# Both heads' scores in one step, alternating RWKV products, and HGRN2 levels over 128 sources in a two-layer hybrid decoder trunk

## The chip, the cores and the metric

The kernel runs on one core of one Trainium2 chip, as one launch. The metric is the device time of that core in microseconds, the median of several runs. TensorE (PE) multiplies matrices into PSUM, VectorE (DVE) and ScalarE (ACT) work elementwise, GpSimd (POOL) does a few powers and clears, SyncE (SP) issues most of the DMAs.

## The reference

The input is one sequence of 256 tokens by 2048 features in fp32; the trunk has two layers. A layer normalises its input, multiplies it by one combined input projection, runs four groups of 8 heads of 64 features on the result, joins the groups by an output projection, and then runs a SwiGLU feed-forward network (2048 to 5632 and back). Both halves have a norm before and after and a residual. The groups are these:

- **Retention** (RetNet): rotary queries and keys, scores `q k` under a causal decay, scores times values.
- **HGRN2**: a gated linear recurrence. Its scores are

```python
pair = jnp.where(causal, jnp.exp(jnp.minimum(cum[:, :, :, None, :] - cum[:, :, None, :, :], 0.0)), 0.0)
scores = jnp.einsum('bhtd,bhsd,bhtsd->bhts', qc, kc, pair)
```

  so every pair of a target t and a source s has a decay of its own in every feature.
- **mLSTM**: scores `q k` times `exp(logd - m_t)`, with stabilised gates, and a normaliser beside the values.
- **RWKV-7**: a generalised delta rule with one state of 64 by 64 a head:

```python
state = (state * jnp.exp(lwt)[:, :, None, :]
         - jnp.einsum('bhvk,bhk->bhv', state, kkt)[..., None] * (at * kkt)[:, :, None, :]
         + vt[..., None] * kt[:, :, None, :])
return state, jnp.einsum('bhvk,bhk->bhv', state, rt)
```

## The kernel before

**Projections.** All weights are streamed from HBM once, in units of 128 x 1024 elements. `Weights` (line 220 on) loads a unit, ScalarE rounds it to `w_hi` (line 246), and VectorE makes the rest `w_lo` (line 247); splitting runs three units ahead (`NHL`). A product is then made of three TensorE passes in a rounded fp32 format, `w_hi` with `u` and with its low part, `w_lo` with `u`. These are the rows named `acc<-u,w_hi`, `po<-w_lo,m` and so on. All matmuls of the kernel go through the helper `mm`, so they have line 299, and transposes have line 303: rows are told apart by their tiles.

**Mixers.** A pair of heads shares the 128 partitions: head 0 on partitions 0 to 63, head 1 on 64 to 127. There are four such tiles j in each group and layer. The mixers are written as Python generators, `rwkv`, `rw_head`, `rw_tail` for RWKV and `retention`, `hgrn`, `mlstm` for the others (the last three groups run one half group after the other, two tiles at once, in the order of `SEQ`). `interleave` (line 723) is the planner: it walks the projection matmuls in `stream` and, wherever a generator is due, lets it issue its next step. Due times are counted in `self.pe`, the planner's own sum of matmul times, and a generator says by `yield 1.1`, say, how much of it must pass before its next step. Within these steps, the build's scheduler orders each engine's instructions by a simulated timeline, so an instruction that is not ready there lets others pass.

**PSUM.** The eight banks are three for projections (`acc`), two for RWKV (`pr`, handed out in turn by `ret_bank`) and three for the other mixers (`po`, by `oth_bank`). A bank that is handed out again must first have been read out by VectorE or ScalarE.

**The places the change touches.**

- `scores` (line 955) makes one head's 128-source scores: a matmul of 256 target columns for the sources 0 to 127 and one of 128 columns for the rest, with 64 contraction rows. `retention` and `mlstm` call it once a head, with a `yield` between.
- `mlstm` (line 1216) first spreads one row of running maxima over 128 partitions by a matmul of `pick` (64 rows, one column broadcast) with `mrow` (64 x 256): the rows `po<-mlrow,mlpick`. Two operations on VectorE subtract the gate and an exponential on ScalarE gives the decay `Dt`, which is multiplied into the scores.
- `hgrn` (line 1079) builds the scores by levels m = 1, 2, 4 ... 64: a level adds all pairs whose source lies in an even block of m tokens and whose target lies in the odd block behind it, and then folds the decays of its blocks into `q2` and `k`. Up to m = 32 a level has four matmuls, for 64 sources (32 at m = 32) on one half of the output partitions each; VectorE copies what the mask `hm` selects into `P` (line 1118, `copy_predicated`), for m up to 16. At 32 and 64 ScalarE and VectorE copy quarters into place.
- `rwkv` (line 1394) makes the triangular products `BK` with `KVR` head by head into two banks. At its end it makes the outputs `y2` head by head: for each of four chunks n of 64 tokens a product of `G` with `KVT` (128 contraction rows, 64 outputs) and, for n above 0, one of `KVR` with the state `S0` (64 rows, 64 outputs).
- `attend` (line 941) multiplies `P` with the values; `P` has three blocks of 128 targets a head.

Of the kernel before, what the change touches and what calls it, by code (L numbers as in the profile page):

```python
# [18 lines left out]
F32R = mybir.dt.float32r  # L19
# [13 lines left out]
LAT = 1.1  # L33
# [70 lines left out]
HMASK = HLEV[:-2]  # L104


def _constants():
# [31 lines left out]
    tg = lambda m: t64[:, t64[0] // m % 2 == 1]  # L139
    hm = np.stack([np.tile(i // m + 1 == tg(m) // m, 2) for m in HMASK], axis=1)  # L140
# [130 lines left out]
class Trunk:  # L271
# [394 lines left out]
    def mixing(self):  # L666
        tc, nc, A, l = self.tc, self.nc, self.A, self.l
        with ExitStack() as ctx:
# [4 lines left out]
            if l == 0:  # L673
                self.W.advance()
                self.c = self.cp.tile([128, NCST - 128], F32, name="cst")
                nc.sync.dma_start(out=self.c, in_=A["cst"][:, 128:])
                self.hm = self.cp.tile([128, len(HMASK), 64], U32, name="hm")
                nc.sync.dma_start(out=self.hm, in_=A["hmask"])
# [262 lines left out]
    def attend(self, P, v, j, nw=None):  # L941

        pso = self.oth_bank()
        for t in range(2):
            for hh in range(2):
                o, h = slice(64 * hh, 64 * hh + 64), 64 * (2 * (j % 2) + hh)
                if t == 0:
                    self.mm(pso[o, 0:256], v[:, 0, h:h + 64], P[:, hh, 0:256], stop=False)
                else:
                    self.mm(pso[o, 128:256], v[:, 1, h:h + 64], P[:, hh, 256:384], start=False)  # L950
# [4 lines left out]
    def scores(self, q, k, hh):  # L955

        r = slice(64 * hh, 64 * hh + 64)
        ps = self.oth_bank()
        self.mm(ps[:, 0:256], k[r, 0:128], q[r, 0:256])
        self.mm(ps[:, 256:384], k[r, 128:256], q[r, 128:256])  # L960
        return ps

    def oth_tiles(self, t):
# [13 lines left out]
        self.mrow = t([64, 256], "mlrow", F32R)  # L977
        self.act(self.mrow.rearrange("p (a b) -> p a b", b=64), self.zero[0:64].unsqueeze(1).to_broadcast([64, 4, 64]))
        self.pick = t([64, 8], "mlpick", F32R)
        self.tt(self.pick, self.ident[0:64, 0:8], self.ident[0:64, 32:40], ALU.add)  # L980
# [30 lines left out]
    def retention(self, j, qk, v, out):  # L1011
        P, rc = self.P[j % 2], self.rcs[j % 2]
        for hh in range(2):
            ps = self.scores(qk[:, 0, :], qk[:, 1, :], hh)
# [4 lines left out]
            yield LAT if hh else 0.5  # L1019
# [59 lines left out]
    def hgrn(self, j, st, v, out):  # L1079
# [8 lines left out]
        D4 = P[:, :, 128:256].rearrange("p h (t c) -> p h t c", t=2)  # L1088
        side = P.rearrange("p h (b t) -> p h b t", b=3)[:, :, 0:3:2, :]
# [10 lines left out]
        self.mul(D4, self.cst("id64", 64).unsqueeze(1).unsqueeze(1).to_broadcast([128, 2, 2, 64]),  # L1100
                 rc[:, 24:28].rearrange("p (t h) -> p h t", t=2).unsqueeze(3).to_broadcast([128, 2, 2, 64]))
        yield LAT
        E, spare = f, e
        for i, m in enumerate(HLEV):
            nb, w = 128 // m, min(m, 32) if m < 64 else 64
            qv = q2.rearrange("p h (b two m) -> p h b two m", two=2, m=m)
            ps = self.oth_bank()
            if m < 64:
                rows = 64 if m < 32 else 32
                o = ps[:, 0:128].rearrange("p (h t c) -> p h t c", h=2, t=2)  # L1110
# [4 lines left out]
                if m < 32:  # L1115
                    dst = P[:, :, 128:256].rearrange("p h (g two m) -> p h g two m", two=2, m=m)[:, :, :, 1, :]
                    mask = self.hm[:, i, :].rearrange("p (g m) -> p g m", m=m)
                    nc.vector.copy_predicated(dst, mask.unsqueeze(1).to_broadcast([128, 2, 64 // m, m]),
                                              ps[:, 0:128].rearrange("p (h g m) -> p h g m", h=2, m=m))
                else:  # L1120
                    for b in range(2):
                        bs = slice(64 * b, 64 * b + 64)
                        (self.act if b else nc.vector.tensor_copy)(side[bs, :, :, bs], D4[bs])
                        self.act(side[64 * b:64 * b + 32, :, :, 64 * b + 32:64 * b + 64], o[64 * b:64 * b + 32])
            else:
                o = ps[0:64, 0:256].rearrange("p (h t c) -> p h t c", h=2, t=2)
                for t in range(2):
                    self.mm(o[:, :, t, :], k[:, 128 * t:128 * t + 64], q2[:, :, 128 * t + 64:128 * t + 128])
                self.act(side[0:64, :, :, 64:128], o)
# [11 lines left out]
        self.act(P[:, :, 128:256], ps[:, 0:256].rearrange("p (h t) -> p h t", h=2))  # L1141
        yield LAT
        self.attend(P, v, j, self.pcol("hg_nw", j))
# [72 lines left out]
    def mlstm(self, j, qk, v, out):  # L1216
        P, rc = self.P[j % 2], self.rcs[j % 2]
        Dt = self.A2[2 * (j % 2) + 1].rearrange("p a t -> p (a t)")[:, 0:384]
        for hh in range(2):
            h = 2 * j + hh  # L1220
            pm = self.oth_bank()
            self.mm(pm[:, 0:256], self.pick[:, h:h + 1].to_broadcast([64, 128]), self.mrow)
            mp = self.cst("mpos", 384)
# [371 lines left out]
```

## Time and profile before

| | |
|---|---|
| median of 3 runs | 2680.61 us (2678.51 to 2680.84) |
| profiled execution | 2681.49 us, span 2679.7 us |
| TensorE, matmul rows | 2630.9 us, 98%, 17732 rows |
| VectorE | 1698.9 us, 63% |
| ScalarE | 1308.2 us, 49% |
| DMA | 459.04 MB, mean 171 GB/s |
| token mixing with its output projection | about 15 to 591 us and 1346 to 1931 us |
| feed-forward | about 599 to 1340 us and 1938 to 2670 us |

How to read it: a timeline row gives the start in us, the time until the last merged instruction ended, the engine, the line, the operation, `out<-in`, the contraction rows * output columns of the stationary operand, the moving operand's size, and how many instructions are merged. An fp32 matmul has two rows in the trace. Matmul rows overlap, since each lasts from its start until its result is out; what counts for the time is the distance from start to start.

### The profile page before, as it was taken

What the parts mean: (1) busy time and instruction counts of PE and PEld (TensorE: products, weight loads), DVE (VectorE), ACT (ScalarE), POOL (GpSimd) and SP (SyncE); (2) the same over time, 40 slices, a digit from 0 to 9 for tenths busy, and PEclk for the clock granted to TensorE, in tenths of its full rate; (3) what the DMA queues carried; (4) which work ended last, traced back from release to release, by engine and by line L of the source; (5) the groups of instructions that cost most, each with busy time, mean ns of one, the idle gap of its engine ahead of it and who ended that gap; (6) DMA issues with size and microseconds to landing.
All of it is one profiled execution on the core that took longest, in us unless ns stands there. A gap on an engine that the chain in (4) does not pass through costs nothing.

```text
span 2679.7 us, 44884 instructions
## 1 busy us (share of the span) xinstructions
PE 2630.9 (98%) x17732; PEld 2352.7 (88%) x17732; DVE 1698.9 (63%) x3017; ACT 1308.2 (49%) x2169; POOL 67.2 (3%) x129
## 2 busy tenths in 40 slices
PE   7999999999999999999999999999899999999998
PEld 7999999888888888888899999997788888888888
DVE  6877877576555555455578778775765555555444
ACT  5454444466444444444374544544564444444442
POOL 0000000000000000000000000000000000000000
PEclk9999999999999999999999999999899999999999
DMA  6544354556666666666555444545466666666664
GB/s 228 160 136 143 118 154 143 161 167 188 189 188 189 188 188 188 192 199 199 171 164 155 137 135 129 155 141 157 140 187 188 188 188 188 188 189 194 195 203 142
DMA packets 149459, 459.04 MB, mean 171 GB/s; under 512 B 29120, under 2 KB 40064, under 8 KB 149248
## 3 DMA queue, kind: packets, MB, share of 16 engines
q1 hardware_dynamic: 148576, 455.51, 56.5%
q8 instruction: 139, 2.28, 0.3%
q10 hardware_dynamic: 672, 0.66, 0.1%
q14 instruction: 72, 0.59, 0.1%
HBM read 450.61 MB, written 3.41 MB: 169 GB/s over the span
## 4 chain that ended last, share of the span: by engine, by line
PE 98%; DVE 1%; ACT 0%; DMA 0%; issue 0%; POOL 0%; SPq 0%; POOLq 0%; DVEq 0%; ACTq 0%
PE acc L299 56%; PE po L299 28%; PE pr L299 13%; PE pr L303 1%; PE po L303 1%; DVE h L291 0%; DMA h<-in_x 0%; DVE un L287 0%; POOL small L309 0%; SPq L340 0%; ACT junk L294 0%; DVE w_lo L247 0%; DVE u L291 0%; DVE small L291 0%; DVE yw L291 0%
## 5 line engine op out<-in xcount | busy, mean ns | idle before, releaser
L247 DVE TENSOR_TENSOR w_lo<-w_raw,w_hi 128x1024 fp32r<-128x1024 f32 x840 | 1028.2, 1224 | 756.4 <-ACT w_hi L246 745.8
L246 ACT ACTIVATE w_hi<-w_raw 128x1024 fp32r<-128x1024 f32 x840 | 889.0, 1059 | 979.2 <-PE po L299 339.8
L299 PE MATMUL acc<-u,w_hi 128*128 128x256 f32 (+1 forms) x4256 | 999.1, 315 | 0.9 <-DVE u L291 0.9
L299 PE MATMUL acc<-u,w_lo 128*128 128x256 f32 x2656 | 750.0, 284 | 1.1 <-DVE w_lo L247 1.1
L299 PEld LDWEIGHTS acc<-u,w_hi 128*128 128x128 f32 x4256 | 701.5, 191 | 55.9 <-issue 3.3
L299 PEld LDWEIGHTS acc<-u,w_lo 128*128 128x128 f32 x2656 | 505.9, 191 | 7.8 <-DVE w_lo L247 1.3
L299 PE MATMUL po<-u,w_hi 128*128 128x512 f32 x1056 | 384.2, 396 | 0.0
L299 PE MATMUL po<-u,w_lo 128*128 128x256 f32 x1056 | 289.8, 279 | 0.0
L299 PE MATMUL pr<-u,w_hi 128*128 128x512 f32 x704 | 245.6, 396 | 0.0
L299 PEld LDWEIGHTS po<-u,w_hi 128*128 128x128 f32 x1056 | 196.6, 188 | 44.5
L299 PEld LDWEIGHTS po<-u,w_lo 128*128 128x128 f32 x1056 | 199.2, 189 | 3.7
L299 PE MATMUL pr<-u,w_lo 128*128 128x256 f32 x704 | 192.5, 279 | 0.0
L299 PE MATMUL acc<-w_hi,ah 128*128 128x256 f32 (+1 forms) x528 | 177.4, 336 | 0.0
L299 PE MATMUL acc<-w_lo,ah 128*128 128x256 f32 (+1 forms) x528 | 177.4, 336 | 0.0
L299 PE MATMUL acc<-w_hi,al 128*128 128x256 f32 (+1 forms) x528 | 177.4, 336 | 0.0
L299 PEld LDWEIGHTS pr<-u,w_hi 128*128 128x128 f32 x704 | 130.3, 188 | 29.4
L299 PE MATMUL acc<-w_hi,u 128*128 128x256 f32 (+1 forms) x768 | 150.3, 290 | 0.0
L299 PEld LDWEIGHTS pr<-u,w_lo 128*128 128x128 f32 x704 | 132.6, 188 | 2.1
L299 PE MATMUL po<-w_hi,ah 128*128 128x512 f32 (+1 forms) x352 | 127.6, 362 | 0.0
L299 PE MATMUL po<-w_hi,al 128*128 128x512 f32 (+1 forms) x352 | 127.6, 362 | 0.0
L299 PE MATMUL po<-w_lo,ah 128*128 128x512 f32 (+1 forms) x352 | 127.6, 362 | 0.0
L299 PEld LDWEIGHTS acc<-w_hi,u 128*128 128x128 f32 x768 | 120.8, 190 | 4.4 <-issue 2.7
(293 smaller groups left out, 2978.1 us busy)
## 6 DMA issues: line engine op xcount, KB each, us to landing
w_raw<-in_wgu SPq DMA_DIRECT2D x352, 512.0 KB, 4.6
w_raw<-in_win SPq DMA_DIRECT2D x240, 512.0 KB, 4.1
w_raw<-in_wdn SPq DMA_DIRECT2D x132, 512.0 KB, 3.8
w_raw<-in_wout SPq DMA_DIRECT2D x48, 512.0 KB, 3.7
w_raw<-in_wdnn SPq DMA_DIRECT2D x44, 512.0 KB, 3.5
w_raw<-in_woutn SPq DMA_DIRECT2D x16, 512.0 KB
w_raw<-in_wmv SPq DMA_DIRECT2D x8, 544.0 KB, 4.2
bp<-in_bpost SPq DMA_DIRECT2D x32, 128.0 KB, 3.2
```

The source lines that it names most:

```text
L246: self.nc.scalar.activation(hi, t, AF.Copy)
L247: self.nc.vector.tensor_tensor(out=lo, in0=t, in1=hi.bitcast(F32), op=ALU.subtract)
L299: self.nc.tensor.matmul(out, lhsT=lhsT, rhs=rhs, start=start, stop=stop, skip_group_check=True)
L303: self.nc.tensor.transpose(out, a, self.ident[0:n, 0:n])
```

## The change

- `scores` makes both heads at once, into two banks, with the matmuls of head 0 and head 1 alternating. `retention` and `mlstm` call it once a tile, and their waits are joined.
- `mlstm` spreads both heads' rows into one bank first, from `mrow` and `pick` of 128 rows (the rows from 64 on are zero), keeps the decay in `P` itself and makes one exponential of both heads.
- `hgrn` makes every level with two matmuls for all 128 sources, and copies all seven levels by the mask, which now has 128 columns. The copies at 32 and 64 and the clear of a quarter of `P` are gone; the diagonal is written for 256 columns a head. The blocks of `P` are in another order, which `attend` takes into account by `last`.
- `rwkv` alternates the heads in the triangular products, into two banks. It makes the outputs of both heads together: first all eight products with `G`, then all six with `S0`, in an order in which neighbours lie on different halves.

```diff
-HMASK = HLEV[:-2]
+HMASK = HLEV
...
-    tg = lambda m: t64[:, t64[0] // m % 2 == 1]
-    hm = np.stack([np.tile(i // m + 1 == tg(m) // m, 2) for m in HMASK], axis=1)
+    t128 = np.arange(128)[None, :]
+    tg = lambda m: t128[:, t128[0] // m % 2 == 1]
+    hm = np.stack([np.tile(p[:, None] // m + 1 == tg(m) // m, 2) for m in HMASK], axis=1)
...
-    def scores(self, q, k, hh):
-        r = slice(64 * hh, 64 * hh + 64)
-        ps = self.oth_bank()
-        self.mm(ps[:, 0:256], k[r, 0:128], q[r, 0:256])
-        self.mm(ps[:, 256:384], k[r, 128:256], q[r, 128:256])
+    def scores(self, qk):
+        ps = [self.oth_bank() for _ in range(2)]
+        for o, s, t in ((slice(0, 256), slice(0, 128), slice(0, 256)), (slice(256, 384), slice(128, 256), slice(128, 256))):
+            for hh in range(2):
+                r = slice(64 * hh, 64 * hh + 64)
+                self.mm(ps[hh][:, o], qk[r, 1, s], qk[r, 0, t])
         return ps
...
-        self.mrow = t([64, 256], "mlrow", F32R)
+        self.mrow = t([128, 256], "mlrow", F32R)
...
-        self.pick = t([64, 8], "mlpick", F32R)
+        self.pick = t([128, 8], "mlpick", F32R)
...
     def retention(self, j, qk, v, out):
-        for hh in range(2):
-            ps = self.scores(qk[:, 0, :], qk[:, 1, :], hh)
+        for hh, ps in enumerate(self.scores(qk)):
...
-            yield LAT if hh else 0.5
+        yield LAT + 0.5
...
     def hgrn(self, j, st, v, out):
-        with self.behind_norm():
-            nc.gpsimd.memset(side[64:128, :, :, 0:64], 0.0)
...
-                for t in range(2):
-                    for b in range(2):
-                        c, g0 = 128 * t + 64 * b, (128 * t + 64 * b) // (2 * m)
-                        self.mm(o[64 * b:64 * b + rows, :, t, :], k[:, c:c + rows], qv[:, :, g0:g0 + 32 // m, 1, :])
...
+            o = ps[:, 0:256].rearrange("p (h t c) -> p h t c", h=2, t=2)
+            for t in range(2):
+                self.mm(o[:, :, t, :], k[:, 128 * t:128 * t + 128], qv[:, :, 64 // m * t:64 // m * (t + 1), 1, :])
+            dst = P[:, :, 0:256].rearrange("p h (g two m) -> p h g two m", two=2, m=m)[:, :, :, 1, :]
+            mask = self.hm[:, i, :].rearrange("p (g m) -> p g m", m=m)
+            nc.vector.copy_predicated(dst, mask.unsqueeze(1).to_broadcast([128, 2, 128 // m, m]),
+                                      ps[:, 0:256].rearrange("p (h g m) -> p h g m", h=2, m=m))
...
     def mlstm(self, j, qk, v, out):
-        for hh in range(2):
-            h = 2 * j + hh
-            pm = self.oth_bank()
-            self.mm(pm[:, 0:256], self.pick[:, h:h + 1].to_broadcast([64, 128]), self.mrow)
...
-            self.act(Dt, Dt, AF.Exp, scale=-1.0)
-            yield 0.8
-            ps = self.scores(qk[:, 0, :], qk[:, 1, :], hh)
-            self.stt(P[:, hh, :], ps[:, 0:384], HD ** -0.5, Dt, ALU.mult, ALU.mult)
-            yield LAT + 0.5 if hh else 1.0
+        pm = self.oth_bank()
+        for hh in range(2):
+            self.mm(pm[:, 256 * hh:256 * hh + 256], self.pick[:, 2 * j + hh:2 * j + hh + 1].to_broadcast([128, 128]), self.mrow)
...
+        self.act(P, P, AF.Exp, scale=-1.0)
+        yield 1.6
+        for hh, ps in enumerate(self.scores(qk)):
+            self.stt(P[:, hh, :], ps[:, 0:384], HD ** -0.5, P[:, hh, :], ALU.mult, ALU.mult)
+        yield LAT + 1.0
...
     def rwkv(self, j, out):
+        pg = [self.ret_bank() for _ in range(2)]
+        for n in range(4):
+            for hh in range(2):
+                rhs = KVR[half[hh], n, 0:3:2, :] if hh == 0 else KVR[half[hh], n, 1:3, :]
+                self.mm(pg[hh][:, 128 * n:128 * n + 128], BK[half[hh], n].rearrange("p s t -> p (s t)"), rhs)
         for hh in range(2):
-            ps = self.ret_bank()
-            for n in range(4):
-                rhs = KVR[half[hh], n, 0:3:2, :] if hh == 0 else KVR[half[hh], n, 1:3, :]
-                self.mm(ps[:, 128 * n:128 * n + 128], BK[half[hh], n].rearrange("p s t -> p (s t)"), rhs)
...
-        for hh in range(2):
-            y2 = self.ret_bank()[:, 0:128].rearrange("p (t e) -> p t e", t=2)
-            for n in (2, 3, 0, 1):
-                o = y2[half[n % 2], n // 2, :]
-                self.mm(o, G[:, hh, n, 64:128], KVT[:, n, hh, :], stop=n == 0)
-                if n > 0:
-                    self.mm(o, KVR[half[hh], n, 2, :], S0[half[hh], n, :], start=False)
+        y2 = [self.ret_bank()[:, 0:128].rearrange("p (t e) -> p t e", t=2) for _ in range(2)]
+        place = lambda n, hh: y2[hh][half[n % 2], n // 2, :]
+        for n, hh in ((0, 0), (1, 0), (0, 1), (1, 1), (2, 0), (3, 0), (2, 1), (3, 1)):
+            self.mm(place(n, hh), G[:, hh, n, 64:128], KVT[:, n, hh, :], start=n < 2, stop=n == 0)
+        for n, hh in ((2, 0), (3, 1), (2, 1), (3, 0), (1, 1), (1, 0)):
+            self.mm(place(n, hh), KVR[half[hh], n, 2, :], S0[half[hh], n, :], start=False)
```

More of the change, by code (lines that the diff above doesn't have):

```diff
@@ L676, in mixing @@
                 nc.sync.dma_start(out=self.c, in_=A["cst"][:, 128:])
-                self.hm = self.cp.tile([128, len(HMASK), 64], U32, name="hm")
+                self.hm = self.cp.tile([128, len(HMASK), 128], U32, name="hm")
                 nc.sync.dma_start(out=self.hm, in_=A["hmask"])
@@ L939, in finish, with attend @@
         self.mul(out, t1, psb[:, 0:256])
-    def attend(self, P, v, j, nw=None):
+    def attend(self, P, v, j, nw=None, last=2):
         pso = self.oth_bank()
+        P3 = P.rearrange("p h (b t) -> p h b t", b=3)
         for t in range(2):
@@ L947, in attend @@
                 if t == 0:
-                    self.mm(pso[o, 0:256], v[:, 0, h:h + 64], P[:, hh, 0:256], stop=False)
+                    self.mm(pso[o, 0:256], v[:, 0, h:h + 64], P3[:, hh, 0:2] if last == 2 else P3[:, hh, 0:3:2], stop=False)
                 else:
-                    self.mm(pso[o, 128:256], v[:, 1, h:h + 64], P[:, hh, 256:384], start=False)
+                    self.mm(pso[o, 128:256], v[:, 1, h:h + 64], P3[:, hh, last], start=False)
         sq, t1, _ = self.scr[j % 2]
@@ L975, in oth_tiles @@
         self.ms = t([128, 6, 16], "mlstats")
[L977 to L980 removed]
+        self.mrow = t([128, 256], "mlrow", F32R)
+        self.act(self.mrow.rearrange("p (a b) -> p a b", b=64), self.zero.unsqueeze(1).to_broadcast([128, 4, 64]))
+        self.pick = t([128, 8], "mlpick", F32R)
+        self.tt(self.pick, self.ident[:, 0:8], self.ident[:, 32:40], ALU.add)
         self.mlv = t([128, 2, 4, 65], "mlv")
@@ L1085, in hgrn @@
         P, rc = self.P[j % 2], self.rcs[j % 2]
-        D4 = P[:, :, 128:256].rearrange("p h (t c) -> p h t c", t=2)
-        side = P.rearrange("p h (b t) -> p h b t", b=3)[:, :, 0:3:2, :]
-        with self.behind_norm():
-            nc.gpsimd.memset(side[64:128, :, :, 0:64], 0.0)
+        near = P[:, :, 0:256].rearrange("p h (t c) -> p h t c", t=2)
         for hh in range(2):
@@ L1099, in hgrn @@
         nc.vector.tensor_copy(rc[:, 24:28], ps[:, 0:4])
-        self.mul(D4, self.cst("id64", 64).unsqueeze(1).unsqueeze(1).to_broadcast([128, 2, 2, 64]),
-                 rc[:, 24:28].rearrange("p (t h) -> p h t", t=2).unsqueeze(3).to_broadcast([128, 2, 2, 64]))
+        self.mul(near, self.ident.unsqueeze(1).unsqueeze(1).to_broadcast([128, 2, 2, 128]),
+                 rc[:, 24:28].rearrange("p (t h) -> p h t", t=2).unsqueeze(3).to_broadcast([128, 2, 2, 128]))
         yield LAT
@@ L1104, in hgrn @@
         for i, m in enumerate(HLEV):
-            nb, w = 128 // m, min(m, 32) if m < 64 else 64
+            nb = 128 // m
             qv = q2.rearrange("p h (b two m) -> p h b two m", two=2, m=m)
             ps = self.oth_bank()
-            if m < 64:
-                rows = 64 if m < 32 else 32
-                o = ps[:, 0:128].rearrange("p (h t c) -> p h t c", h=2, t=2)
-                for t in range(2):
-                    for b in range(2):
-                        c, g0 = 128 * t + 64 * b, (128 * t + 64 * b) // (2 * m)
-                        self.mm(o[64 * b:64 * b + rows, :, t, :], k[:, c:c + rows], qv[:, :, g0:g0 + 32 // m, 1, :])
[L1115 to L1129, printed above, removed]
+            o = ps[:, 0:256].rearrange("p (h t c) -> p h t c", h=2, t=2)
[5 more added lines that the diff above has]
+                                      ps[:, 0:256].rearrange("p (h g m) -> p h g m", h=2, m=m))
             Ev = E[:, 0:2 * nb].rearrange("p (b two) -> p b two", two=2)
@@ L1140, in hgrn @@
         self.mm(ps[:, 0:256], k[:, 0:128], q2[:, :, 128:256])
-        self.act(P[:, :, 128:256], ps[:, 0:256].rearrange("p (h t) -> p h t", h=2))
+        self.act(P[:, :, 256:384], ps[:, 0:256].rearrange("p (h t) -> p h t", h=2))
         yield LAT
-        self.attend(P, v, j, self.pcol("hg_nw", j))
+        self.attend(P, v, j, self.pcol("hg_nw", j), last=1)
         yield LAT
```

12 lines of the change are left out of this document (6 added, 6 removed).

## Prediction, made before the result was known

> **What bounds the kernel now.** I read the page first, then the waits of TensorE, then the busy times of the two token-mixing stretches.
>
> ```profile
> span 2679.7 us, 44884 instructions
> PE 98%; DVE 1%; ACT 0%; DMA 0%; issue 0%; POOL 0%; SPq 0%; POOLq 0%; DVEq 0%; ACTq 0%
> PE po L303 <- DVE un L287: 27.9, 5, 13.0
> PE pr L303 <- DVE kap L287: 3.2, 1, 3.2
> PE acc L299 <- DVE w_lo L247: 1.1, 1, 1.1
> sum 840.00, PE 840.00 PEld 787.93 DVE 653.99 ACT 414.43 POOL 45.74; mean PE 420.00 PEld 393.96 DVE 326.99 ACT 207.21 POOL 22.87
> HBM read 450.61 MB, written 3.41 MB: 169 GB/s over the span
> ```
>
> The chain that ended last is TensorE for 98% of the span. Its largest wait, 27.9 us for `un`, lies at the norms, which the change does not touch. For split weights (`w_lo`) it waited 1.1 us in all. The sum row is over both token-mixing stretches (60 to 480 and 1400 to 1820): TensorE is busy without a gap, VectorE 654 of 840 us, ScalarE half. So the projection matmuls always have their operands, and every mixer block between them pushes them back by its own length. A TensorE microsecond saved in a block is a microsecond of span, as long as VectorE keeps up.
>
> **How a block is priced.** A block is a run of mixer matmuls between two projection matmuls. Each fp32 matmul leaves two records. The timeline of TensorE around one head's RWKV output products:
>
> ```profile
> 190.61 0.28 PE L299 MATMUL acc<-u,w_hi 128*128 128x256 f32 x1
> 190.82 0.33 PE L299 MATMUL pr<-KVT,G 128*64 128x64 f32 x2
> 191.08 0.33 PE L299 MATMUL pr<-S,KVR 64*64 64x64 f32 x2
> ...
> 191.85 0.34 PE L299 MATMUL pr<-KVT,G 128*64 128x64 f32 x4
> 192.37 0.39 PE L299 MATMUL acc<-u,w_hi 128*128 128x256 f32 x1
> 192.59 0.28 PE L299 MATMUL acc<-u,w_lo 128*128 128x256 f32 x1
> 243.44 0.68 PE L299 MATMUL pr<-TDD,LoT 64*64 64x64 f32 x16
> 244.05 0.44 PE L303 MATMUL po<-ident,A 128*128 128x128 f32 x2
> ```
>
> Projection matmuls of 256 columns start 0.12 us apart. Here the block starts 0.21 after the last one (0.09 too late), and the first one after it takes 0.22 (0.10 too much): a block of another tile shape costs 0.19 besides its own length. This head: 192.37 − 190.82 + 0.19 = 1.74 us. It has 14 records, but 0.26 passes from group to group, with two records or four: it pays for its five changes of shape, not for work. The last two rows are the opposite: 16 records of one shape, heads alternating, take 0.61, so a step of two records costs about 0.06.
>
> **RWKV output products** (end of `rwkv`). Two heads, four tiles, two layers: 16 blocks of 1.74 now, 3.48 a tile. The change issues 8 products with `G` (16 records, neighbours in different column halves), then 6 with `S0` (12 records, different row halves), into two banks. By the 16-record row: 0.61 + (0.61 − 2 × 0.06) + 0.19 = 1.29, so 2.19 saved a tile, 17.5 us over eight. Where the last chunk's values come late the block will break in two and pay entry, exit and a shape change again; I take half the tiles broken at about 0.25 each: **−16.5**. Lower bound: if the second bank is not free, each head goes alone with its own products grouped, two runs near 0.39 (the 8-record row below) + 0.19 = 0.97, 1.94 a tile: −12.3. The last tile of layer 1 also stands on the chain ahead of the 3.2 us wait for `kap`; it gains the same there.
>
> **RWKV's triangular products** (`BK` with `KVR`), heads alternating instead of one after the other:
>
> ```profile
> 93.64 1.71 PE L299 MATMUL pr<-KVR,BK 64*128 64x128 f32 x16
> 95.28 0.39 PE L299 MATMUL acc<-u,w_lo 128*128 128x256 f32 x1
> 54.68 0.70 PE L299 MATMUL pr<-X,wa 64*128 64x256 f32 x4
> 55.31 0.51 PE L299 MATMUL acc<-u,w_hi 128*128 128x256 f32 x2
> 169.04 0.70 PE L299 MATMUL pr<-X,wa 64*128 64x256 f32 x2
> 169.66 0.39 PE L299 MATMUL acc<-u,w_lo 128*128 128x256 f32 x1
> ```
>
> `X,wa` is the test that the kernel already contains: two matmuls on different row halves into two banks. Together, four records take 0.63; one alone takes 0.62. The second head is free when it stands beside the first. In the triangular block 16 records take 1.64. At 0.11 a record (full-shape rows below) plus 0.2 of filling and draining they would need 1.96 in a row, so about three of eight steps overlap already; alternating needs 8 × 0.11 + 0.2 = 1.08. Saved 0.56 × 8 = 4.5 at most, nothing if the second bank comes late; both heads stand in one block now, so I take **−4.0**.
>
> The Trainium skill, TensorE: Matmul & The Clock Gate, Part 3, says that matmuls keep program order in start and end. By that rule two heads issued one after the other would share nothing, and alternating would save 8 × 0.11 = 0.88 a tile, 7.0 us. The 1.64 here is too short for it, so the row decides.
>
> **Scores and decay rows.**
>
> ```profile
> 224.47 0.92 PE L299 MATMUL po<-A 64*128 64x256 f32 x4
> 225.32 0.39 PE L299 MATMUL acc<-w_lo,u 128*128 128x256 f32 x1
> 225.75 0.38 PE L299 MATMUL po<-mlrow,mlpick 64*128 64x256 f32 x1
> 226.06 0.39 PE L299 MATMUL acc<-w_hi,u 128*128 128x256 f32 x1
> 480.39 0.93 PE L299 MATMUL po<-A 64*128 64x256 f32 x8
> 481.25 0.39 PE L299 MATMUL acc<-u,w_lo 128*128 128x256 f32 x1
> ```
>
> The first is one mLSTM head, 0.85 + 0.19 = 1.04. The x8 row is a retention pair whose two heads already run side by side in 0.86 + 0.19 = 1.05. So retention has most of this gain: **−0.8**, between 0 and −1.6. For mLSTM's eight pairs, 2 × 1.04 becomes 1.05 where both banks are free: 8.2 us at most. But the ring has three banks, the decay rows of both running pairs take two of them, and each head's bank must first be read out by VectorE (four operations a pair). Where one head comes first, the schedule sends it alone, as in the `X,wa` row at 169.04. I take a third: **−2.5**, between 0 and −8.2.
>
> The decay rows (`mlpick`) go from 64 to 128 rows, the shape of the projections: 0.31 + 0.19 = 0.50 alone now, afterwards 0.12 like a projection matmul. Some stand beside scores and cost less, so I put the sixteen at 0.38: **−4.2**, between −3 and −6.1. In exchange the exponential now waits for both heads' four operations on VectorE; behind it on ScalarE stand the `w_hi` of later units, and ScalarE has half its time free.
>
> **HGRN2's levels.** Now four matmuls a level on 64 column halves, 8 records; afterwards two on the full shape, 4 records.
>
> ```profile
> 109.92 0.46 PE L299 MATMUL po<-A,A 128*64 128x64 f32 x8
> 110.31 0.50 PE L299 MATMUL acc<-u,w_hi 128*128 128x256 f32 x2
> 139.42 0.65 PE L299 MATMUL po<-A,A 128*64 128x128 f32 x4
> 140.00 0.39 PE L299 MATMUL acc<-w_hi,u 128*128 128x272 f32 x1
> 155.68 0.38 PE L299 MATMUL pr<-KVT,KBT 128*128 128x128 f32 x2
> 155.90 0.38 PE L303 MATMUL po<-ident,A 128*128 128x128 f32 x2
> 156.04 0.38 PE L299 MATMUL acc<-w_lo,u 128*128 128x272 f32 x1
> 156.26 0.41 PE L299 MATMUL acc<-w_hi,u 128*128 128x272 f32 x2
> ```
>
> A small level costs 0.39 + 0.19 = 0.58 alone; the level of 64 costs 0.58 + 0.19 = 0.77. Four full-shape fp32 records cost 0.36 and, with no late entry, 0.09 after them (0.22 in place of 0.13, these projections having 272 columns): 0.45, 0.11 each in the array. With 0.55 for six levels (two pairs' levels sometimes share a block) a pair now pays 4.07 and will pay 7 × 0.45 = 3.15: **−7.4** over eight pairs; between 0 (levels always shared) and −8.8.
>
> What VectorE gets in exchange:
>
> ```profile
> L1118 DVE COPY_PREDICATED P<-hm,po x40: 278/301/496, 113.0 to 1618.1; 128x128 f32<-128x128 uint32 x40
> L278 DVE TENSOR_TENSOR P<-cst,rc x8: 404/412/420, 112.0 to 1600.0; 128x256 f32<-128x256 f32 x8
> L1123 DVE COPY P<-P x8: 276/278/281, 132.1 to 1619.4; 64x256 f32<-64x256 f32 x8
> sum 158.00, PE 158.00 PEld 142.40 DVE 136.95 ACT 65.63 POOL 2.27; mean PE 39.50 PEld 35.60 DVE 34.24 ACT 16.41 POOL 0.57
> ```
>
> The last row sums the four stretches in which the small levels run (109 to 145, 266 to 312, 1437 to 1473, 1593 to 1633): VectorE is busy 137 of 158 us. The masked copies go from 5 of 128 columns a pair, about 0.35 each, to 7 of 256. Their price is bounded by 0.35 + 0.14 = 0.49 (an estimate: the tensor operations' slope per 128 columns) and by twice, 0.70. With the copy of 0.28 gone and the diagonal doubled (0.41 to about 0.68) that adds 8 × 1.7 = 13 to 8 × 3.1 = 25 us, while TensorE leaves 7.4 less: 150 to 162 us of work in 150.6. At the lower price it just fits; at the upper 11.5 us are missing. What is late next is `w_lo`, three units ahead. I take **+3**, between 0 and +11.5.
>
> Costed at nothing: the fewer ScalarE copies and the dropped clear on GpSimd, which are off the chain, and the zero rows of `mlrow`, written before the first projection ends. The mask grows from 160 to 448 KB on SP's queue; behind it stand `wa`, `gup`, `gb` and the later weight units. The units requested ahead of it cover it; at the mean rate of 169 GB/s it would cost 1.7 us once without them. The planner charges an fp32 matmul by 4 × max(rows out, columns), which comes to the same per level, per score and per product before and after, so the projections keep their places beside the mixers.
>
> **The sum.** −16.5 − 4.0 − 0.8 − 2.5 − 4.2 − 7.4 + 3 = −32.4 us. The profiled execution took 2681.5 (span 2679.7): 2649.1. It stands 0.9 above the median of 2680.6, so the forecast is **2648**. All upper bounds without the VectorE loss give −46.7, 2634.
>
> **Rivals.**
> 1. *The second bank is late everywhere*: alternation exists only in the program's text. Rows at 169.04 speak for it, the x8 and x4 rows against. Scores and triangular products gain nothing, the output products only their grouping: −12.3 − 4.2 − 7.4 + 3 = −20.9, 2660.
> 2. *VectorE becomes the bound in the HGRN2 stretches* at 0.70 a copy: −35.4 + 11.5 = −23.9, 2657. For it: 137 of 158; against it: `w_lo` waits of 1.1.
> 3. *The late entry and exit belong to fp32, not to the shape*; then full-shape levels pay 0.19 too and give up the column halves. The array's own time doubles from 4 steps of 0.06 to 4 of 0.11 on 48 levels, +0.2 × 48 = 9.6 in place of −7.4: −15.4, 2665. The row at 155.90 speaks against it. The Trainium skill, TensorEngine Tiling (Array Packing), Performance Considerations, points this way: with a stationary free size up to 64 it wants column tiling.
> 4. *Slower*: the masked copy of 256 columns from PSUM costs far more than twice. The 56 copies are in VectorE's order ahead of `w_lo`. The need is 137 + 56c − 14 (what is dropped of today's copies, net of the diagonal) against 150.6; it eats the whole 35.4 from c = 1.13 us; at 1.25 the shortage is 42, +7, 2688. Nothing in the copies' 0.28 to 0.50 suggests it.
>
> **How the numbers follow.** Forecast 0.63, rivals 0.17, 0.11, 0.06 and 0.03. The range 2632 to 2664 reaches from the upper bounds past rivals 1 and 2. Faster by over 0.2%, about what a measurement of this kernel tells from no change: 0.96; within: 0.01, between rivals 3 and 4; slower: 0.03, rival 4.
>
> **What would show it.** Output products in blocks of some 28 records near 1.1 us, not two of 1.55; `mlpick` rows of 128*128 without a late entry; level rows of 128*128 x4; `KVR,BK` near 1.1. If mLSTM's `po<-A` rows stay x4, the banks were late. If TensorE waits for `w_lo` appear in the four stretches, rival 2 or 4 holds. A copy above 0.7, or new waits over 10 us elsewhere, would make the prediction wrong.

## The result and the profile after

| | before | after |
|---|---|---|
| median | 2680.32 us (2678.51 to 2680.84) | 2666.59 us (2664.78 to 2668.22) |
| span of the profiled execution | 2679.7 us | 2664.2 us |
| TensorE, matmul rows | 2630.9 us, 17732 | 2608.6 us, 17540 |
| VectorE | 1698.9 us | 1705.3 us |
| ScalarE | 1308.2 us | 1297.5 us |

The change makes the kernel faster: the ratio is 0.995, with an interval of 0.9933 to 0.9967, or 13.7 us. The forecast was 32.4 us, and the time lies 2.6 us above the end of the range. A layer's token mixing, with its output projection, can be counted from the wait for `un` that opens the layer to the wait for `un` behind its output projection (12.95 to 585.81 and 1334.62 to 1924.80 us in before, 12.42 to 584.89 and 1333.13 to 1909.54 in after). So counted, layer 1 became 13.8 us shorter and layer 0 only 0.4, although both run the same code. Something in layer 0 eats most of what the parts gain there.

The chain of waits in after, by engine:

```profile
PE 96%; DVE 2%; DMA 1%; issue 0%; ACT 0%; POOL 0%; SPq 0%; POOLq 0%; DVEq 0%; ACTq 0%
```

TensorE's share of the chain falls from 98 to 96%; VectorE's rises from 1 to 2 and that of DMA from 0 to 1%. The waits of TensorE in after (line, tile, what it waited for, us in total, how often, the longest):

```profile
PE po L304 <- DVE un L288: 27.8, 7, 12.4
PE pr L304 <- DVE kap L288: 7.0, 2, 3.8
PE acc L300 <- ACT m L295: 4.4, 2, 2.2
PE acc L300 <- DVE w_lo L248: 1.0, 2, 0.8
PE pr L300 <- DVE KVT L287: 0.9, 2, 0.5
```

and the row of the same view of before that the prediction doesn't show:

```profile
PE acc L299 <- ACT m L294: 2.2, 1, 2.2
```

The norms' wait for `un` is what it was, and `w_lo` is in time. But `kap` and `m` were waited for once and are now waited for twice: before, this pair of waits stood in layer 1 alone. The windows around the end of the mixers show the same (us, busy time of TensorE, weight loads, VectorE, ScalarE, GpSimd, granted TensorE clock, DMA share, GB/s), first before, in layer 0 and in layer 1:

```profile
480.00:560.00 80.00, 80.00 (x405) 65.56 (x405) 46.99 (x85) 38.15 (x70) 5.64 (x5) 1.00 0.58 169
1840.00:1880.00 40.00, 33.84 (x159) 26.77 (x158) 18.53 (x30) 13.90 (x23) 1.48 (x2) 0.87 0.50 145
```

then after, in layer 0 and in layer 1:

```profile
480.00:560.00 80.00, 72.82 (x356) 60.15 (x355) 40.46 (x75) 33.89 (x65) 3.95 (x5) 0.94 0.51 149
1780.00:1870.00 90.00, 83.42 (x512) 67.85 (x511) 49.63 (x89) 38.02 (x60) 3.94 (x5) 0.94 0.50 145
```

In layer 0, TensorE worked through the 80 us before; now it is idle for 7.2 of them, at a mean clock of 0.94. The timeline of TensorE in after at that place (start, length, the wait and its releaser in brackets; a few rows are enough):

```profile
526.26 0.39 PE L300 MATMUL po<-w_lo,m 128*128 128x512 f32 x1
526.49 0.62 PE L300 MATMUL po<-w_hi,m 128*128 128x512 f32 x2
526.94 0.40 PE L300 MATMUL po<-w_lo,m 128*128 128x512 f32 x1
...
527.82 0.43 PE L300 MATMUL pr<-F,TT 128*128 128x64 f32 x2 [0.31 <-DVE F L279]
...
529.77 0.45 PE L300 MATMUL pr<-KVT,G 128*64 128x64 f32 x8 [0.50 <-DVE KVT L287]
...
535.44 0.66 PE L304 MATMUL pr<-ident,kap 128*128 128x128 f32 x2 [3.77 <-DVE kap L288]
538.32 1.65 PE L300 MATMUL acc<-w_hi,m 128*128 128x512 f32 x3 [2.21 <-ACT m L295]
...
541.47 0.63 PE L300 MATMUL acc<-w_lo,m 128*128 128x512 f32 x1
541.90 0.63 PE L300 MATMUL acc<-w_hi,m 128*128 128x512 f32 x1
...
542.70 0.63 PE L300 MATMUL acc<-w_hi,m 128*128 128x512 f32 x2
```

From 526.94 to 538.32 no projection matmul starts; this is the dry stretch, as it is called from here on. TensorE does the last steps of the last RWKV tile one after the other, each of which waits for an elementwise operation on its result. The output projection needs that tile in its last units and has nothing else to do. The chain of work through the same place, in order of time:

```profile
528.23 1.23 DVE w_lo L248
529.49 0.24 DVE KVT L287
529.77 0.84 PE pr L300 x14
...
533.46 1.05 POOL rwc L310
534.53 0.77 DVE kap L288 x3
```

The last two rows belong to `rw_tail`: mean and variance, a power on GpSimd, the scalings of `kap`, then the transposes. A weight split of 1.23 us even stands in VectorE's order ahead of the last `KVT`. The wait isn't all of the price. The windows give the granted clock (the figure after GpSimd's):

```profile
529.00:532.00 3.00, 1.79 (x22) 1.05 (x20) 1.56 (x5) 0.53 (x3) 0.00 (x0) 1.00 0.59 198
532.00:533.00 1.00, 0.00 (x0) 0.00 (x0) 0.00 (x0) 1.00 (x8) 0.00 (x0) 0.69 0.49 197
535.00:542.00 7.00, 4.34 (x11) 3.28 (x12) 2.71 (x7) 1.15 (x2) 0.00 (x0) 0.50 0.00 0
```

The clock falls from 1.00 to 0.50 between 532 and 533 us, early in the wait of 3.77 us: TensorE's last row ended at 531.68 (530.98 + 0.70), and in the 3 us before 532 it was busy for 1.79. It is still 0.50 when the work comes back, and projection matmuls that started 0.23 us apart (526.26, 526.49) start 0.43 apart (541.47, 541.90) until 542.70. The Trainium skill, TensorE: Matmul & The Clock Gate, Part 1, says that the clock is halved after an idle window of about 3.4 us and comes back after about as long a time of sustained work. The trace agrees on the way back, with 4.4 us of matmuls at half clock after 538.32; on the way down it does not, for no idle stretch of 3.4 us stood ahead of the fall. By an estimate from these rows the dry stretch costs about 10 us: 11.4 us without a projection matmul, less some 3 of mixer work that had to be done anyway, plus about 2 for ten matmuls at half clock.

Why it is late is seen in the order. The build fixes TensorE's order, and the trace repeats it. Projection and feed-forward matmuls that stand ahead of the first transposes of the tail of the last RWKV tile:

| | layer 0 | layer 1 |
|---|---|---|
| the place where the projection must wait for it | 3192 | 10784 |
| before | 3167 | 10784 |
| after | 3192 | 10784 |

In before, 25 projection matmuls (some 5.7 us) were left to cover that tail in layer 0. In after there are none, as in layer 1 of both kernels.

The last tile is not the only late one, and 25 is not the whole delay, since no tail can stand behind the place where the projection waits for it. Counted in the same way, the four tails of layer 0 stand at 1328, 1934, 2599 and 3167 in before and at 1358, 2028, 2749 and 3192 in after. The third shows what single parts do to the chain. In the kernels below that have one part alone it stands at 2599 with the outputs or the decay rows, 2647 with the triangular products, 2660 with scores and decay rows, and 2666 with the levels.

The parts themselves, in after. RWKV's output products of one tile:

```profile
414.61 0.45 PE L300 MATMUL pr<-KVT,G 128*64 128x64 f32 x6
...
417.58 0.33 PE L300 MATMUL pr<-KVT,G 128*64 128x64 f32 x2
417.84 0.45 PE L300 MATMUL pr<-S,KVR 64*64 64x64 f32 x6
...
419.71 0.45 PE L300 MATMUL pr<-KVT,G 128*64 128x64 f32 x8
420.09 0.44 PE L300 MATMUL pr<-S,KVR 64*64 64x64 f32 x6
420.46 0.39 PE L300 MATMUL acc<-w_hi,u 128*128 128x256 f32 x1
```

The products are grouped, but the heads do not share a stretch. Head 0 goes in two pieces and head 1 alone behind it, in six of the eight tiles. In the last tile of each layer no projection matmul lies between them, but head 1 still comes behind head 0, in layer 0 after the wait of 0.50 us for `KVT` shown above. With entry and exit they take 0.57, 0.83 and 0.95, together 2.35 us a tile; the kernel before took 3.48, and the forecast wanted 1.29 plus a break in half the tiles.

The other parts: a triangular block with its successor, an mLSTM head, a level and a pair of decay rows with their neighbours, the masked copy, and the sum over the four HGRN2 stretches of 109 to 145, 266 to 312, 1437 to 1473 and 1593 to 1633:

```profile
423.76 1.16 PE L300 MATMUL pr<-KVR,BK 64*128 64x128 f32 x16
424.86 0.39 PE L300 MATMUL acc<-u,w_hi 128*128 128x256 f32 x1
404.33 0.92 PE L300 MATMUL po<-A 64*128 64x256 f32 x4
125.96 0.28 PE L300 MATMUL acc<-u,w_lo 128*128 128x256 f32 x1
126.08 0.60 PE L300 MATMUL po<-A,A 128*128 128x128 f32 x4
126.44 0.48 PE L300 MATMUL acc<-u,w_hi 128*128 128x256 f32 x2
399.03 0.28 PE L300 MATMUL acc<-u,w_lo 128*128 128x256 f32 x1
399.14 0.40 PE L300 MATMUL po<-mlrow,mlpick 128*128 128x256 f32 x2
399.38 0.39 PE L300 MATMUL acc<-u,w_hi 128*128 128x256 f32 x2
L1114 DVE COPY_PREDICATED P<-hm,po 128x256 f32<-128x256 uint32 x56 | 29.0, 518 | 2.9 <-PE po L300 2.4
sum 158.00, PE 157.72 PEld 153.32 DVE 144.36 ACT 62.45 POOL 2.94; mean PE 39.43 PEld 38.33 DVE 36.09 ACT 15.61 POOL 0.74
```

Sixteen alternating triangular records take 1.10 (before 1.64; three of the eight blocks stayed at 1.42, and one took 1.64 as before). A level takes 0.36 in the array and enters without delay, 0.12 after the projection matmul ahead of it. Two decay rows take 0.24, the pace of projection matmuls. The x4 row is a lone mLSTM head; two of mLSTM's eight pairs came together, the other six stayed apart. The masked copy costs 518 ns in the mean, near the lower bound, and VectorE is busy 144 of 158 us in the HGRN2 stretches.

### The profile page after: what moved, and what is told of

It is laid out like the page before. It is cut to its first block, busy times and chain, and to the rows that moved or that the text cites. A ratio compares the mean times of both kernels' runs of the same rounds, so it can differ in the third digit from the quotient of the medians.

```text
span 2664.2 us, 44425 instructions
## 1 busy us (share of the span) xinstructions
PE 2608.6 (98%) x17540; PEld 2344.9 (88%) x17540; DVE 1705.3 (64%) x3025; ACT 1297.5 (49%) x2129; POOL 63.9 (2%) x121
## 4 chain that ended last, share of the span: by engine, by line
PE 96%; DVE 2%; DMA 1%; issue 0%; ACT 0%; POOL 0%; SPq 0%; POOLq 0%; DVEq 0%; ACTq 0%
PE acc L300 55%; PE po L300 28%; PE pr L300 12%; DVE w_lo L248 1%; PE pr L304 1%; PE po L304 0%; DVE h L292 0%; DVE un L288 0%; DMA h<-in_x 0%; DVE A L279 0%; DMA bp<-in_bpost 0%; DMA XD<-kap 0%; POOL small L310 0%; SPq L341 0%; ACT junk L295 0%
```

## The experiments

Theory A: the parts are worth roughly their rows, but in layer 0 the RWKV chain comes later in TensorE's order, and the projection runs dry. Rival B: the larger masked copies keep VectorE busy and hold up the chain. Rival C: the parts are worth half. Every time below is a median; the kernel before stood at 2679.5 to 2681.3 beside them.

### The dependence cut in layer 0

```diff
-                    self.act(self.mh[i], self.mx[key])
-                    self.tt(self.ml[i], self.mx[key], self.mh[i].bitcast(F32), ALU.subtract)
+                    src = self.mx["rw", 0] if self.l == 0 and key == ("rw", 1) else self.mx[key]
+                    self.act(self.mh[i], src)
+                    self.tt(self.ml[i], src, self.mh[i].bitcast(F32), ALU.subtract)
```

> The changed kernel, but in layer 0 the output projection no longer waits for the last RWKV pair: the split of the mixed rows into high and low halves reads the first RWKV pair once more in the place of the second. Left out: the second RWKV pair's values in layer 0's output projection; all of its own work is still done. Theory A (the RWKV chain of layer 0 comes 25 projection matmuls later on TensorE, the projection then runs dry for 7.0 + 4.4 us and works at a low clock after it): the stretch at 527 to 538 us closes and the time falls by about 10 us from the 2666.6 of the changed kernel, to 2656 (2653 to 2660). Rival B (the larger masked copies of HGRN2 keep VectorE busy and hold up all of the chain): the copies stay, so the time stays at 2665 to 2668. Rival C (the parts are simply worth half of what the rows gave): also 2665 to 2668.

Measured: 2658.14 us, ratio 0.9919 (0.9904 to 0.9934). The window in layer 0 is full again, at full clock, and the waits for `kap` and `m` are down to layer 1's:

```profile
480.00:560.00 80.00, 80.00 (x437) 68.22 (x436) 48.00 (x94) 41.87 (x89) 3.94 (x5) 1.00 0.61 179
PE pr L304 <- DVE kap L288: 3.8, 1, 3.8
PE acc L300 <- ACT m L295: 2.2, 1, 2.2
```

With the dry stretch gone the kernel takes 8.5 us less. In layer 0 alone, from `un` to `un`, it is 9.8; layer 1 became 1.6 longer, and its wait for `kap` 0.5. C leaves no room for this. Of B it says less than the text above claims: a chain that the copies held up would be cut off in the same way. So the cut shows the price of the dry stretch, not what makes the chain late. It also shows how late the chain is: with nothing waiting for it, the last tail of layer 0 stands at 3301.

### Scores head by head again

The decay rows keep 128 partitions; the rest is the changed kernel:

```diff
-        for hh, ps in enumerate(self.scores(qk)):
+        for hh in range(2):
+            ps = self.scores(qk[:, 0, :], qk[:, 1, :], hh)
...
+            yield LAT if hh else 0.5
-        yield LAT + 0.5
```

(`retention`; `scores` and `mlstm` likewise as before, but with `pick` and `mrow` of 128 rows.)

> The changed kernel with the scores of retention and mLSTM head by head as before (the decay rows picked from 128 partitions stay, and so do HGRN2, the triangular products and the outputs). In this build the last RWKV tile of layer 0 has its tail 3167 projection matmuls into the layers as before, and not 3192. Theory A: outputs -10, triangular products -2.9, decay rows -4.2, levels -6.5, no dry stretch: 2680.3 - 23.6 = 2657 (2654 to 2660), faster than the changed kernel though it does less of the change. Rival B (the copies of HGRN2): they stay, so 2666 or above. Rival C (parts worth half): 2668.

Measured: 2660.71 us, 0.9927 (0.991 to 0.9943): 5.9 us faster than the whole change with less of it done. Layer 0's wait is gone, with the tail at 3167. The time is 3.7 us above what the sum of rows gave, so some part was still overrated.

### HGRN2's old levels

```diff
-HMASK = HLEV
+HMASK = HLEV[:-2]
```

(with `hgrn`, `attend` and the mask as before.)

> The changed kernel with HGRN2's levels as before; scores, decay rows, triangular products and outputs as changed. In this build the tail of layer 0's last RWKV tile still stands at 3192 projection matmuls. Theory A: the dry stretch stays, and the levels' 6.5 us are lost: 2666.6 + 6.5 = 2673 (2670 to 2676). Rival B (the copies cause the loss): without them the loss of about 11 us goes and 6.5 come back: 2662 or below. Rival C (levels worth half): 2669.5.

Measured: 2671.66 us, 0.9966 (0.9953 to 0.9979), 5.1 us slower than the changed kernel. The waits for `kap` and `m` stay at two each. So the dry stretch of layer 0 is there without the larger copies, and B falls as its only cause. The levels are worth 5.1 here, somewhat less than the 6.5 of their blocks. The levels do delay the chain, though (2666 in place of 2599 for the third tail, alone), and whether their copies do it or their matmuls is not shown.

### The output products alone

The kernel before with the new order of `y2` and nothing else.

> The kernel before with the RWKV output products alone as changed. The order leaves head 0's products in front of head 1's, in stretches of their own. Theory A (a tile then takes 2.3 us beside 3.6 before, eight tiles): -10, so 2670 (2668 to 2672). The forecast's step (both heads in one stretch, -16.5): 2664. Its lower bound (-12.3): 2668.

Measured: 2669.69 us, 0.9958 (0.9943 to 0.9973), −10.9 us. This is the head-by-head price, not the forecast's.

### Both heads in one stretch

What holds head 1 back is its last `KVT`, which VectorE writes in its order behind a weight split. One line gives both halves of the last chunk to ScalarE:

```diff
-            self.ts(KVT[half[1], n, 1, :], ps[half[1], 0:64], -1.0)
+            if n == 3:
+                self.act(KVT[half[1], n, 1, :], ps[half[1], 0:64], AF.Copy, scale=-1.0)
+            else:
+                self.ts(KVT[half[1], n, 1, :], ps[half[1], 0:64], -1.0)
```

> The kernel before with the RWKV output products as changed, and one line more: for the last chunk (n = 3) both halves of KVT are written by ScalarE, where one was VectorE's. Then the order of this build puts the products of both heads into one stretch, and the tails of the last RWKV tile stand earlier: 3155 in place of 3167 matmuls in layer 0, and 10760 in place of 10784 (where the projection stands still) in layer 1. Theory A: outputs -16.5 (the forecast's step, now with both heads together), and layer 1's dry stretch of 3.2 + 2.2 us with the low clock behind it gone, about -8: 2680.5 - 24.5 = 2656 (2653 to 2659). Rival (heads together are worth no more than head by head): 2669.7 of the outputs alone, less the dry stretch: 2661.5. Rival (a dry stretch isn't tied to the order): 2663.

Measured: 2653.95 us, 0.9899 (0.9885 to 0.9914), −27.1 us for the outputs and one line. A tile's products (timeline of TensorE), and the windows of both layers' ends:

```profile
393.96 0.45 PE L299 MATMUL pr<-KVT,G 128*64 128x64 f32 x6
...
397.16 0.56 PE L299 MATMUL pr<-KVT,G 128*64 128x64 f32 x10
397.66 0.46 PE L299 MATMUL pr<-S,KVR 64*64 64x64 f32 x12
398.05 0.38 PE L299 MATMUL acc<-u,w_lo 128*128 128x256 f32 x1
480.00:560.00 80.00, 80.00 (x434) 67.04 (x433) 48.56 (x91) 42.84 (x89) 3.62 (x4) 1.00 0.59 178
1780.00:1870.00 90.00, 90.00 (x529) 75.90 (x528) 54.01 (x90) 45.18 (x80) 5.03 (x5) 1.00 0.56 169
```

The second piece holds ten records with `G` and twelve with the state in 0.89; with the first piece, entries and exits a tile takes 0.57 + 1.08 = 1.65 us. The tails stand earlier (3155 and 10760), and neither layer runs dry: of all waits for `kap` and `m` none is left. The line brought 15.7 us, of which at most 8 × (2.35 − 1.65) = 5.6 are the products; the rest goes with the dry stretch of layer 1, which the kernel before has too. The layers say the same: beside the outputs alone, layer 0 became 2.5 us shorter and layer 1 13.0.

### The best of the parts

That kernel with the triangular products alternating and the decay rows picked from 128 partitions.

```diff
-        self.pick = t([64, 8], "mlpick", F32R)
+        self.pick = t([128, 8], "mlpick", F32R)
...
-        for hh in range(2):
-            ps = self.ret_bank()
-            for n in range(4):
+        pg = [self.ret_bank() for _ in range(2)]
+        for n in range(4):
+            for hh in range(2):
```

> The kernel of one block (outputs as changed, the last KVT halves both on ScalarE) with the triangular products alternating and the decay rows picked from 128 partitions; scores and HGRN2's levels as before. The tails stand at 3155 and 10760 as there. Theory A: 2656 - 2.9 - 4.2 = 2649 (2646 to 2653). Rival (the parts take from each other): 2655 or above.

Measured: 2649.08 us, 0.9881 (0.9866 to 0.9896), faster than both kernels.

### Each part alone

The kernel before with the levels alone.

> The kernel before with HGRN2's levels alone as changed. The RWKV chain of layer 0 comes some 30 projection matmuls later at its second and third tile, but the last tail stands at 3167 as before. Theory A: by the rows of after -6.5, so 2674 (2672 to 2676). Rival B (the larger copies hold up the chain): 2680 or above. The changed kernel with old levels was 5.0 us slower than with new ones, which would make it 2675.5.

Measured: 2675.28 us, 0.9978 (0.9968 to 0.9987), −5.8 us. A copy takes 522 ns here too.

The kernel before with both groups' scores and the decay rows.

> The kernel before with the scores of retention and mLSTM for both heads in one step, and the decay rows picked from 128 partitions. The last tail of layer 0 stands at 3167 as before. Theory A: -4.2 from the decay rows, -1.5 from the scores: 2675 (2673 to 2677). Rival (the scores by themselves are the loss, whatever the place of the tail): 2680 or above.

Measured: 2678.29 us, 0.9993 (0.9983 to 1.0002): −2.8 us, less than the decay rows alone were expected to give.

The kernel before with the triangular products alone.

> The kernel before with the triangular products alone as changed. The tail of layer 0 stands at 3168, beside 3167 before. By the eight stretches of after, -2.9: 2677.5 (2676 to 2679.5). The forecast's step: -4.0, 2676.5. Rival (the chain comes later by as much as the products save): 2680.5.

Measured: 2682.10 us, 1.0001 (0.9991 to 1.001): nothing. Its eight blocks are 3.1 us shorter together (four at 1.61 and four at 1.28 with entry and exit, beside eight at 1.83), but the order of the rest has changed too. TensorE's waits show a new one, longer than the gain:

```profile
PE pr L299 <- DVE TDD L278: 4.3, 2, 2.8
1695.00:1697.00 2.00, 2.00 (x11) 2.00 (x11) 1.17 (x5) 0.00 (x0) 1.58 (x2) 0.50 0.09 16
```

The second row, a window, adds to it: the wait of 2.8 us in layer 1 ended at 1693.7, and after it TensorE worked at half clock. Layer 1 became 3.1 us longer, layer 0 stayed as it was.

The kernel before with the decay rows alone.

> The kernel before with the decay rows alone picked from 128 partitions. Every tail stands where it stood before. The forecast's step: -4.2, 2676.3 (2675 to 2678). Rival (the row's own time beside neighbours of another shape eats the gain): 2680. With the kernel of all score parts at 2678.3, a value of 2676.3 here means that the joint scores by themselves cost 2 us.

Measured: 2675.52 us, 0.9979 (0.9969 to 0.9989), −5.8 us. Beside the −2.8 above, the joint scores by themselves would cost some 3 us rather than save any; the two intervals overlap a little, so neither the size nor the sign is settled.

### One line more in the changed kernel

The changed kernel with the line for the last `KVT`.

> The changed kernel with the one line more (both halves of KVT of the last chunk on ScalarE), so that the output products of both heads share a stretch in the six tiles where they stood apart; the two last tiles had them together already. The tails still stand at 3192 and 10784, where the projection waits. Theory A: 6 x (2.3 - 1.65) = -4, so 2662.5 (2661 to 2665), and both dry stretches remain. Rival (the earlier KVT closes the dry stretches as well): 2650.

Measured: 2665.06 us, 0.9938 (0.9923 to 0.9953): −1.5 us, just outside what A allowed, and −2.5 when each kernel is set against the kernel before that was measured beside it. The interval overlaps that of the changed kernel (0.9933 to 0.9967), so a gain is not shown. Six tiles do share a stretch now (0.88 us). In the two last tiles, which the text above takes to be together already, head 1 still comes behind head 0. The waits for `kap` add up to 7.5 us there, 7.0 in the changed kernel: where the chain sets the end, TensorE's time saved ahead of it can turn into a longer wait.

### The levels on top of the best

> The kernel of 2649.1 us with HGRN2's levels as changed, that is the changed kernel plus the one line, less the joint scores. Alone, the levels took 5.8 us off the kernel before. In this build they put the tails of both layers back to 3192 and 10784. Theory A (a part that is worth time on TensorE costs more than that where it makes the RWKV chain late): 2649.1 - 5.8 + 2 x 8.5 = 2660 (2656 to 2663), slower. Rival (parts add up): 2643.

Measured: 2661.68 us, 0.9925 (0.9911 to 0.994). A part that takes 5.8 us off the kernel before puts 12.6 us onto this one. Its tails stand at 3192 and 10784, and TensorE waits again at both, in layer 0 for `m` alone:

```profile
PE acc L300 <- ACT m L295: 4.4, 2, 2.2
PE pr L304 <- DVE kap L288: 3.5, 1, 3.5
```

This fits A: the same copies and products are worth time in one kernel and cost it in the other, and the tails have moved. But it speaks for B's mechanism as well, since here it is the levels that make the chain late. And the place of the tails does not set the time alone. The kernel with the scores head by head (2660.71) differs from this one by the `KVT` line only and has its last tail of layer 0 at 3167; its time is the same within the intervals. So the line that went with 15.7 us above brings nothing here.

### What the triangular products and the retention scores are worth where no tail is late

The best kernel without the alternating triangular products:

> The kernel of 2649.1 us with the triangular products head by head as before: outputs in one stretch, decay rows from 128 partitions, nothing else. Tails at 3155 and 10760 as there. Theory A (the 3.4 us that alternating saves in its own stretches are kept where no step of the chain waits): 2649.1 + 3.4 = 2652.5 (2651 to 2654). Theory B (they are lost in the joins with other work and in waits on TDD, as alone): 2649 (2647.5 to 2650). From the parts one by one: 2654.0 of the one block less 5.8 of the rows alone: 2648.

the same with retention's scores joined:

> As e13, with the retention scores of both heads in one step as changed (mLSTM's stay head by head). Its retention pairs stood together in most tiles before, so by the rows -0.4 at most from e13; the tail of layer 0 stands at 3144, 11 matmuls earlier. Theory A: within 1 us of e13. Rival (the joint scores by themselves cost 2 to 3 us, as the kernel of all score parts beside the decay rows alone shows): 2 us or more above e13.

and the best kernel beside them:

> The kernel of 2649.1 us beside e13 and e14 on one chip, for the difference that the triangular products make. Theory A: 3.4 us below e13. Theory B: within 1 us of it.

Measured: 2649.65, 2651.01 and 2647.53 us. The triangular products give 2.1 us here, between the two theories. Joining retention's scores gives nothing and perhaps costs a little (+1.4). The three intervals overlap (0.9872 to 0.9905, 0.9878 to 0.9907, 0.9866 to 0.9896), so both signs are likely but not shown. Another comparison lies in the same runs: the kernel without alternating triangular products is the kernel of one block plus the decay rows. Each beside its own kernel before, they stand at −29.8 and −27.1, so the decay rows are worth some 2.7 us here, half of what they were worth alone, though the two intervals overlap.

## Why the prediction was wrong

It had the direction, and the bound: a microsecond of TensorE in a block is a microsecond of the span, as long as its operands arrive. The steps one by one:

| term | forecast, us | measured, us | from |
|---|---|---|---|
| output products | −16.5 | −10.9 | alone |
| triangular products | −4.0 | −2.9, and 0.8 worse alone | blocks of after; alone |
| scores | −0.8 − 2.5 | about +3 | scores with rows, less rows alone |
| decay rows | −4.2 | −5.8; −2.7 | alone; with the outputs in one stretch |
| levels and VectorE's load | −7.4 + 3 | −5.8 | alone |
| "the projections keep their places" | 0 | +8.5 | the cut |
| sum, with the first figure of each | −32.4 | −13.9 | measured together: −13.7 |

That the sum agrees is luck: a term is uncertain by some 2 us either way and depends on the kernel that it is added to, and the triangular products enter with their blocks. With the 0.8 that they cost alone the sum would be −10.2.

**The step that failed** is the one costed at nothing: "the planner charges ... the same per level, per score and per product before and after, so the projections keep their places beside the mixers". Equal charges did not keep the places. The last RWKV tail of layer 0 came 25 matmuls later (134 where nothing waits for it), and nothing was left to cover it. That cost 8.5 us where nothing was charged. The prediction had the row that warned of it, the wait of 3.2 us for `kap`; it counted the wait as layer 1's and didn't ask how much cover layer 0 still had, some 5.7 us. By the third tail, the levels, the triangular products and, with the decay rows, the joint scores each delay the chain by 48 to 67 matmuls, and all together by 150. Whether the planner or the scheduler does it, and by what rule, is not shown.

**The output products** were mis-sized. The mechanism was right and is seen with 1.65 us a tile in one stretch, but the forecast took the heads to be together in half the tiles and more. In all eight, head 1 came behind head 0, because the two halves of the last `KVT` come from different engines, one of them behind a weight split (1.23 us in the rows above). The kernel with one line more shows it: with both halves on ScalarE the heads share a stretch. The lower bound of −12.3 had head by head, but in one piece each.

**The scores** came near what was assumed in their blocks: two of eight mLSTM pairs together, where a third was taken, and x4 rows elsewhere, as the prediction's own test said they would be if the banks were late. But the time did not follow. The kernel with all score parts came out some 3 us above the one with the decay rows alone, where the prediction allowed 0 to −8.2 for mLSTM and 0 to −1.6 for retention; as the intervals overlap, the loss is likely, and where it would go is not shown.

**Decay rows and levels** had the mechanism right: a level takes 0.36 in the array and a decay row 0.12, with no delay at entry. The decay rows gave 5.8 and 2.7 on either side of the 4.2. Levels and VectorE's load together gave −5.8 where −4.4 was forecast; at 518 ns a copy stays near the lower bound of 0.49, but what the load cost by itself is not shown.

**The rivals.** 3 has the nearest time (2665), by luck: it makes the levels a loss, and they gave −5.8 and enter without delay. 1, the second bank late everywhere (2660), has half of the mechanism: scores gained nothing and the outputs only their grouping, but the lateness of the outputs was VectorE's `KVT`, not a bank, and the triangular products became shorter in seven of eight blocks. 2 and 4 fall with the 518 ns and with the old levels making the changed kernel slower. No rival had the dry stretch of layer 0.

## What to carry to other kernels

A chain of many short steps beside a stream of matmuls is hidden only while matmuls are left behind its last step: count that cover before any change of order, and charge a stretch that runs dry with its waits and with the half clock after them. When planner and scheduler order an engine, equal charges need not keep equal places; compare the orders, not the charges. In this kernel matmuls of two heads shared a stretch once their last operands came from the same engine, and there the copy that was moved went with more time (15.7 us) than the reordering itself (10.9). A part's worth alone is not its worth in another kernel: the levels gave 5.8 us alone and cost 12.6 on top of the best.

## What was not expected of the hardware

- A masked copy of 128 partitions by 256 fp32 columns from PSUM takes 518 ns in the mean (395 to 753), one of 128 columns took 353 before (278 to 496): 165 ns between the means.
- A halved clock does not need a long idle stretch. In after the granted clock fell to 0.50 between 532 and 533 us, when TensorE's last row had ended at 531.68. In the kernel with the triangular products alone a wait of 2.8 us was followed by half clock while TensorE was busy throughout (1695 to 1697). Part of a wait's price is so paid after TensorE has work again: about 2 of the 10 us of the dry stretch, by the estimate above.
- Twenty-two records of output products, of both heads, take 0.89 us in one stretch (397.16 to 398.05); fourteen of one head take 0.75 (419.71 to 420.46). Eight further records cost 0.14 where the matmuls of both heads share the stretch.
